# Turning attention's probabilities and all of x with VectorE and DRAM, and making the output projection's second product whole

## The chip, the cores and the metric

The kernel runs on one core of one Trainium2 chip. A core has five engines that run their own instruction queues side by side: TensorE (PE in the profile) multiplies matrices, VectorE (DVE) and ScalarE (ACT) work element by element, GpSimd (POOL) does small work and issues transfers, and SyncE (SP) issues transfers. 16 DMA engines move data between DRAM and the on-chip memory (SBUF). The metric is the device time of one execution in microseconds (us).

## The reference

One layer of a sequence model: 512 tokens of width 2048, all in float32. A norm, a sliding-window attention with a gate, an output projection, a residual, then a second gated branch and a last norm:

```python
hn = rmsnorm(x, norm_g)
q, k, v, gate = split(hn @ w_in)              # 32 heads of 64, 4 key/value heads
scores = q k^T * 64 ** -0.5 + bias            # blocks of 128 queries, 256 keys, window 128
scores = where(mask, scores, min)
m = maximum(scores.max(-1), sink)
e = exp(scores - m)
probs = e / (e.sum(-1) + exp(sink - m))
y = ((probs @ v) * silu(gate)) @ w_out
x = x + y
emb = p @ ple_proj
g = sigmoid(rmsnorm(x, ple_norm) @ ple_gate)
return rmsnorm(x + emb * g, final_g)
```

## The kernel before

**Every large product in three.** A float32 operand is split into a rounded high part (a cast by ScalarE, `fp32r`) and the rest (a subtraction by VectorE). `mm3` (L123 to L128) then issues three matmuls: high by high, high by low, low by high. Weights come in tiles of 128x1024 (512 KB), loaded by SP, split on ScalarE (L109, L765) and VectorE (L110, L766).

**Start (to about 90 us).** x, turned by the host, is scaled and split; the keys, the values and the first two query chunks are projected.

**The attention loop (about 90 to 445 us).** Two things run side by side. `projections` yields one k-step (a `mm3` of 512 columns) at a time for the remaining 14 query and 16 gate chunks, 16 k-steps each. `kinds` holds their order, and `q_at` says where the query chunks stand in it. 464 k-steps fall into the loop. Attention runs in 64 blocks `i`, one per turn of the loop: block `i = 8 d + g` holds four heads (`d`) and 64 queries (`g`). The generator `scores(i)` multiplies queries with keys, adds the bias, takes the maximum, the exponential and the reciprocal, and scales the probabilities into a tile `pr` (L542), queries on partitions. `turn(i)` has TensorE turn them (L551, two transposes of 128x128 a block, one where g is 0, by the identity `ident`), casts the result out of the bank `pt` into `r` (high part on ScalarE, L564; low part on VectorE, L565), and has POOL cut out the keys of the own block (`own`, L575). `weigh(i)` multiplies by the values and adds the result into `U`. In turn `i` of the loop stand the steps of `scores(i)` and `scores(i - 1)`, `turn(i - 2)` and `weigh(i - 3)`; the loop has 67 turns, and the k-steps are shared out over the first 66. The order within a turn is written out by hand for all five engines (`manual_schedule`): after k-steps 0 to 5 stand the weight splits (`W.todo`), the chores (what follows a finished projection) and the next steps of the generators.

**Sums beside the loop.** The output projection and the later `ple_gate` product are computed with seven products of half size in place of eight (numbers 1 to 7), some of which need sums of weight blocks. These sums are made in DRAM during the loop: SP copies a 512 KB block (L723), POOL adds another onto it with an accumulating transfer (L725). `sums_in(i)` shares out these steps.

**The output projection (about 447 to 620 us).** `unit(p, jj, ...)` makes the half `jj` of product `p`: four weight tiles, each 2 k by 2 banks by 3 matmuls. The order is 1, 7, 6, 5, 3, 4 (`ORDER_OUT`). Product 2 is made apart, by the class `Small`, again with seven products of half size, spread over products 3 and 4 (`SMALL["w_out"]`, `small_steps`). `add_y` adds each bank to the resident `x1` (L1120, L1122). The products of the embedding (`EMBED_AT`) stand in between. VectorE and POOL are not ordered by hand in this part; ScalarE is from product 4 on.

**Turning x.** The `ple_gate` product needs the new x with columns on partitions (`hT`). The quarter j of the columns and half th of the tokens goes one of two ways. For j = 0 and 1 with th = 0, `turn(kp, th, tag)` has TensorE transpose 16 pieces of 128x128 (L1054) at the end of product 4. For the others, `turn_blocks` has VectorE transpose blocks of 32x32 (L1073), POOL writes them to DRAM (L1075), `gather_blocks` reads them back in four transfers with the blocks exchanged (L1083), and `scale_turned` scales them on ScalarE (L1092). `turns_at` places these steps.

**The second branch (about 620 to 780 us)** runs the `ple_gate` products in the order 1, 7, 6, 5, 3, 4, its product 2 by `Small`, then the gate and the last norm.

Of the kernel before, what the change touches and what calls it, by code (L numbers as in the profile page):

```python
# [19 lines left out]
S = 512  # L20
P = 128
# [34 lines left out]
def trunk_kernel(ctx: ExitStack, tc: tile.TileContext, a: dict):  # L56
# [75 lines left out]
    ident = const.tile([P, P], F32, name="ident")  # L132
    make_identity(nc, ident)
# [47 lines left out]
    q_at = {int(0.5 + 3.516 * (c // 2)) - 3 + c % 2: c for c in range(2, PAIRS)}  # L181
# [170 lines left out]
    kt = [kvq.tile([P, S], F32, name=f"kt{t}") for t in range(2)]  # L352
# [116 lines left out]
    def scores(i):  # L469
# [64 lines left out]
        T[i] = operands.tile([P, 2, P], F32, tag="pr", name=f"pr{i}", bufs=3)  # L534
        for u in range(2):
            out, src = T[i][:, u], pr[u]
            if g == 0:
                out = T[i][:, 0, u * HB : (u + 1) * HB]
            if late and (g + u) % 2:
                out = out.rearrange("p (h k) -> p h k", h=2)[:, ::-1]  # L540
                src = src.rearrange("p (h k) -> p h k", h=2)
            nc.scalar.mul(out, src, sm[:, 4 + u : 5 + u])  # L542

    def turn(i):


        d, g = divmod(i, UNITS)
        pr = T.pop(i)
        pt = bank(f"pt{i}", "t")[:, :256]
        for u in range(2 if g else 1):  # L550
            nc.tensor.transpose(pt[:, u * P : (u + 1) * P], pr[:, u, :], ident)  # L551

        r = operands.tile([P, 2, 256], F32R, tag="r", name=f"r{i}", bufs=2)
        rh, rl = (r[:, l].rearrange("p (h u q) -> p u h q", h=4, u=2) for l in range(2))
        src = pt.rearrange("p (u h q) -> p u h q", u=2, h=4)
        if g == 0:
            lower, upper = slice(0, HB), slice(HB, P)
            nc.scalar.copy(rh[lower, 0], src[lower, 0])
            nc.scalar.copy(rl[upper, 1], src[upper, 0])
            nc.vector.tensor_sub(rh[upper, 0], src[lower, 0], rh[lower, 0].bitcast(F32))  # L560
            nc.vector.tensor_sub(rh[upper, 1], src[upper, 0], rl[upper, 1].bitcast(F32))
            nc.scalar.copy(rh[lower, 1], rl[upper, 1].bitcast(F32))
        else:
            nc.scalar.copy(rh, src)  # L564
            nc.vector.tensor_sub(rl, src, rh.bitcast(F32))  # L565
# [21 lines left out]
    def weigh(i):  # L587
# [5 lines left out]
        if g == 0:  # L593
            U[d] = apool.tile([P, 2, S], F32, tag="u", name=f"u{d}", bufs=3)
# [14 lines left out]
        if b:  # L609
            dst = U[d][:, :, n * P : (n + 1) * P].rearrange("p u (b q) -> p b u q", b=2)  # L610
            lower, upper = slice(0, 64), slice(64, 128)
            tmp = [apool.tile([P, 2, 2, HB], F32, tag=f"tmp{e}", name=f"tmp{e}_{i}", bufs=1) for e in range(2)]
            for e, (o, x) in enumerate(((lower, upper), (upper, lower))):
                nc.scalar.copy(tmp[e][o], ops[x, :, :, e, :])
            for e, o in enumerate((lower, upper)):
                nc.vector.tensor_add(dst[o], ops[o, :, :, e, :], tmp[e][o])
# [47 lines left out]
    def blk(t):  # L664
# [4 lines left out]
    ORDER_OUT = ORDER_PLE = (1, 7, 6, 5, 3, 4)  # L669

    SMALL = {
        "w_out": {
            (3, 0): {1: [1], 2: [1], 3: [7]}, (3, 1): {0: [7], 1: [6], 2: [6], 3: [2]},
            (4, 0): {0: [2], 1: [5], 2: [5], 3: [4]}, (4, 1): {0: [4, 3], 1: [3]},
        },
# [132 lines left out]
    def add_stage(nm, order):  # L808
        at = {}

        for p in order:
            for jj in range(2):
                at[p, jj] = []
                for m in range(4):
# [3 lines left out]
                    else:  # L818
                        src = block(nm, *{1: (1, 1), 3: (2, 2), 6: (1, 1), 4: (2, 1)}[p], jj, m)
# [8 lines left out]
                    for q in SMALL[nm].get((p, jj), {}).get(m, ()):  # L828
# [21 lines left out]
    class Forms:  # L850
# [6 lines left out]
        def steps(self, p):  # L857

            self.made[p] = []
            for h in range(2):  # L860
# [5 lines left out]
                    5: (a21, (a21, a22)), 3: (a11, (a12, a11)), 4: (a22, None),  # L866
# [52 lines left out]
    def sums_in(i):  # L919
# [6 lines left out]
        n, of = SUM_STEPS - SUMS_EARLY, blocks - 4  # L926
# [9 lines left out]
    for i in range(blocks + 3):  # L936

        before, softmax = softmax, scores(i) if i < blocks else iter(())
        turned = turn(i - 2) if 2 <= i < blocks + 2 else iter(())
        value = weigh(i - 3) if 3 <= i else iter(())  # L940
        next(turned, None)
# [8 lines left out]
        todo = left // (blocks + 2 - i) if i < blocks + 2 else 0  # L950
        left -= todo
        for n in range(max(todo, 6)):
            if n < todo:
                next(proj)
            if n == 0:
                first_chores(i, 1)
                some(W.todo)
                some(chores or idle)
            elif n == 2:
                next(turned, None)  # L960
                next(value, None)
                if len(chores) > 1:
                    some(chores)
            elif n == 3:
                next(softmax, None)
            elif n == 4:
                first_chores(i, 2)
                some(chores or idle)
            elif n == 5:
                next(softmax, None)  # L970
        if i < blocks:
# [19 lines left out]
    def banks(p, jj, nm):  # L991
# [3 lines left out]
        tag = "sp"[jj] if p != 7 else "to"[jj] if nm == "o" else "t"  # L995
# [48 lines left out]
    def turn(kp, th, tag):  # L1044

        g = kp // 2
        if g not in hT:
            hT[g] = swapped[(g + 2) % 4] = quarter(f"hT{g}")
        tp = bank(f"tp{kp}_{th}", tag)
        for n in range(2):  # L1050
            k = 2 * kp + n
            for tb in range(2):
                src = x1[k // 4][:, 2 * th + tb, (k % 4) * P : (k % 4 + 1) * P]
# [784 lines left out]
```

## Time and profile before

| | us |
|---|---|
| median of three runs | 781.91 (781.47 to 781.96) |
| the profiled execution | 781.41 |
| its span, first to last instruction | 779.70 |

Mean granted TensorE clock in that execution: 0.997. The profile is one execution. Each row of its groups of instructions gives the line of the code, the engine, the operation, what it writes and reads with the shapes, how often, the busy time, the mean of one in ns, and the idle time just before. Rows of stretches give start and end, the length, then for each engine the busy time and in brackets the number of instructions (PE, PEld for the loading of the matrix that stands still, DVE, ACT, POOL), the granted clock, the mean busy share of the DMA engines and GB/s. Rows of the chain and of the order in time give start, length, engine, line, operation. Rows of transfers give what is written and read, the issuing queue, the count, the KB of one and the median us from issue to landing. Rows of waits give who waited for whom, the sum, the count and the longest.

### The profile page before, as it was taken

The page shows a single profiled execution, that of the slowest core. Times are in us where ns is not written, and L with a number is a line of the kernel's source. Part 1 is how long each engine was busy: PE and PEld are TensorE (multiplying, and loading weights), DVE is VectorE, ACT ScalarE, POOL GpSimd, SP SyncE. Part 2 cuts the span into 40 slices and gives each one's busy share as a digit, 9 for nine tenths or more (in the row PEclk, how much of TensorE's full clock was granted, in tenths as well). Part 3 has the DMA queues.
Part 4 walks back from the last instruction along what each step waited for, and adds up shares of the span by engine and source line. Part 5 has one row for each costly group of instructions (what it writes and reads, how often), then busy time and mean ns, then how long its engine had stood idle before and what let it go on. Part 6 is the DMA issues. An engine that isn't in the chain of part 4 may idle for free.

```text
span 779.7 us, 11154 instructions
## 1 busy us (share of the span) xinstructions
PE 770.1 (99%) x3652; PEld 644.1 (83%) x3652; DVE 618.9 (79%) x1069; ACT 529.3 (68%) x1121; POOL 169.8 (22%) x307
## 2 busy tenths in 40 slices
PE   9999999999999999999999999999999999999995
PEld 8888888888888888888888888888888888888884
DVE  4546697876978688777877799968799889999995
ACT  6743586766777676766766664577766888867874
POOL 0201523132232313132332200112101122221111
PEclk9999999999999999999999999999999999999998
DMA  9978899999999999999998588999899999999956
GB/s 343 305 207 301 182 260 311 272 312 258 287 247 278 280 241 278 277 279 277 248 288 218 136 298 313 359 290 290 318 389 337 320 284 295 325 264 309 321 132 216
DMA packets 52858, 217.22 MB, mean 279 GB/s; under 512 B 8112, under 2 KB 9136, under 8 KB 46720
## 3 DMA queue, kind: packets, MB, share of 16 engines
q1 hardware_dynamic: 39280, 156.67, 56.5%
q0 software_dynamic: 13520, 59.83, 36.2%
q8 instruction: 29, 0.48, 0.3%
q14 instruction: 29, 0.24, 0.1%
HBM read 199.65 MB, written 82.89 MB: 362 GB/s over the span
## 4 chain that ended last, share of the span: by engine, by line
PE 98%; issue 1%; DVE 0%; POOL 0%; POOLq 0%; DVEq 0%
PE gps L126 7%; PE gps L127 7%; PE gps L128 7%; PE qps L126 7%; PE qps L128 7%; PE qps L127 7%; PE o L126 6%; PE o L127 6%; PE o L128 6%; PE g L127 5%; PE g L128 5%; PE g L126 5%; PE s L485 2%; PE vps L290 2%; PE o L603 2%; PE pt L551 2%
## 5 line engine op out<-in xcount | busy, mean ns | idle before, releaser
L766 DVE TENSOR_TENSOR blo<-braw,bhi 128x1024 fp32r<-128x1024 f32 x100 | 121.5, 1220 | 20.9 <-ACT bhi L765 19.9
L765 ACT CAST bhi<-braw 128x1024 fp32r<-128x1024 f32 x100 | 105.1, 1052 | 47.1 <-PE o L128 15.1
L126 PE MATMUL gps<-xh,whi 128*128 128x512 f32 x256 | 100.0, 390 | 0.0
L127 PE MATMUL gps<-xl,whi 128*128 128x512 f32 x256 | 99.9, 390 | 0.0
L128 PE MATMUL gps<-xh,wlo 128*128 128x512 f32 x256 | 99.8, 390 | 0.0
L126 PE MATMUL qps<-xh,whi 128*128 128x512 f32 x224 | 87.8, 392 | 0.0
L128 PE MATMUL qps<-xh,wlo 128*128 128x512 f32 x224 | 87.5, 390 | 0.0
L127 PE MATMUL qps<-xl,whi 128*128 128x512 f32 x224 | 87.4, 390 | 0.0
L575 POOL TENSOR_SCALAR_AFFINE_SELECT own<-r 64x512 fp32r<-64x512 f32 (+1 forms) x48 | 32.5, 677 | 238.4 <-DVE r L565 234.4
L110 DVE TENSOR_TENSOR wlo<-wraw,whi 128x1024 fp32r<-128x1024 f32 x60 | 73.5, 1227 | 2.8 <-ACT whi L109 2.7
L126 PE MATMUL o<-bhi,fho 128*128 128x512 f32 x192 | 74.8, 390 | 0.0
L127 PE MATMUL o<-blo,fho 128*128 128x512 f32 x192 | 74.7, 389 | 0.0
L128 PE MATMUL o<-bhi,flo 128*128 128x512 f32 x192 | 74.7, 389 | 0.0
L109 ACT CAST whi<-wraw 128x1024 fp32r<-128x1024 f32 x60 | 62.3, 1040 | 4.6 <-issue 4.1
L126 PE MATMUL g<-bhi,fhg 128*128 128x512 f32 x160 | 62.3, 390 | 0.0
L127 PE MATMUL g<-blo,fhg 128*128 128x512 f32 x160 | 62.2, 389 | 0.0
L128 PE MATMUL g<-bhi,flg 128*128 128x512 f32 x160 | 62.2, 389 | 0.0
L128 PEld LDWEIGHTS gps<-xh,wlo 128*128 128x128 f32 x256 | 48.1, 188 | 10.3
L126 PEld LDWEIGHTS gps<-xh,whi 128*128 128x128 f32 x256 | 48.1, 188 | 9.2
L529 ACT ACTIVATE t<-t,sm 128x129 f32<-128x129 f32 (+1 forms) x128 | 49.6, 389 | 8.7 <-DVE sm L525 7.4
L127 PEld LDWEIGHTS gps<-xl,whi 128*128 128x128 f32 x256 | 48.1, 188 | 8.9
L565 DVE TENSOR_TENSOR r<-pt,r 128x256 fp32r<-128x256 f32 x56 | 23.7, 424 | 38.9 <-ACT r L564 38.1
(299 smaller groups left out, 1827.6 us busy)
## 6 DMA issues: line engine op xcount, KB each, us to landing
wraw<-in_w_gate_in SPq DMA_DIRECT2D x32, 512.0 KB, 8.1
w_out<-in_w_out POOLq DMA_DIRECT2D x32, 512.0 KB, 9.1
braw<-w_out SPq DMA_DIRECT2D x32, 512.0 KB, 8.1
wraw<-in_w_q SPq DMA_DIRECT2D x28, 512.0 KB, 6.7
braw<-in_w_out SPq DMA_DIRECT2D x22, 512.0 KB, 5.7
braw<-in_ple_gate SPq DMA_DIRECT2D x22, 512.0 KB, 6.9
ple_gate<-in_ple_gate POOLq DMA_DIRECT2D x20, 512.0 KB, 8.9
xw<-in_first SPq DMA_DIRECT2D x14, 640.5 KB, 6.5
```

The source lines that it names most:

```text
L109: nc.scalar.copy(hi, raw)
L110: nc.vector.tensor_sub(lo, raw, hi.bitcast(F32))
L126: nc.tensor.matmul(ps, sh, mh, start=first, stop=False, skip_group_check=more)
L127: nc.tensor.matmul(ps, sh, ml, start=False, stop=False, skip_group_check=more)
L128: nc.tensor.matmul(ps, sl, mh, start=False, stop=last, skip_group_check=more)
L290: nc.tensor.matmul(v_ps[t], h[:, c], part_of(high_at, 256, 512), start=f, stop=e, skip_group_check=True)
L485: nc.tensor.matmul(s_ps[:, u, : 2 * n], st, of_keys[:, first * 2 * QB : (first * QB + n) * 2], start=True, stop=True)
L529: nc.scalar.activation(su, su, AF.Exp, bias=sm[:, u : u + 1], accum_out=sm[:, 2 + u : 3 + u])
L565: nc.vector.tensor_sub(rl, src, rh.bitcast(F32))
L575: nc.gpsimd.affine_select(out=flat(own), in_=flat(r).bitcast(F32), pattern=[[0, 8], [sign, HB]], compare_op=ALU.is_ge, fill=0.0, base=-HB ...
L765: nc.scalar.copy(hi[:, :n], raw)
L766: nc.vector.tensor_sub(lo[:, :n], raw, hi[:, :n].bitcast(F32))
```

## The change

In attention, `scores` scales the probabilities in place, and a new last step has VectorE transpose them in 32x32 blocks into a tile `turned`, which holds two blocks of attention (a pair `a`). `send(a)` writes it to DRAM from ScalarE's queue (256 KB). `fetch(a)` reads it back on SP's queue in four transfers of 64 KB, in runs of 512 bytes, with the blocks exchanged, into the tile `back`. `turn(i)` casts `r` out of `back` in place of the bank. `weigh` follows seven turns behind `scores` in place of three; the loop has 71 turns, and the k-steps are shared out over 70. `turned` and `back` have two buffers each; to make room `u` has two buffers in place of three (the keys' tile `both_kt` serves as `u` for d = 6) and `tmp` is one tile. `q_at` moves the query chunks earlier. The transposes by `ident`, and `ident` itself, are gone.

In the output projection, product 2 becomes a whole one between products 3 and 4: 8 weight tiles straight from `w_out`. The small products of `w_out`, their sums in DRAM and their forms are gone; the sums that are left are shared out over 64 turns in place of 60. ScalarE is ordered by hand from product 2 on. x is turned for j = 0 and 1, th = 0 too by `turn_blocks`, `gather_blocks` and `scale_turned`; those for j = 2 and 3 move from product 4 to product 2.

```diff
-    q_at = {int(0.5 + 3.516 * (c // 2)) - 3 + c % 2: c for c in range(2, PAIRS)}
+    q_at = {int(0.5 + 3.333 * (c // 2)) - 3 + c % 2: c for c in range(2, PAIRS)}
...
-        T[i] = operands.tile([P, 2, P], F32, tag="pr", name=f"pr{i}", bufs=3)
         for u in range(2):
-            out, src = T[i][:, u], pr[u]
+            nc.scalar.mul(pr[u], pr[u], sm[:, 4 + u : 5 + u])
+        yield
+
+        a, v = divmod(i, 2)
+        if not v:
+            T[a] = operands.tile([P, 512], F32, tag="turned", name=f"turned{a}", bufs=2)
+        to = T[a].rearrange("p (j v u q) -> p v u j q", j=4, v=2, u=2)[:, v]
+        for u in range(2):
+            out, src = to[:, u], pr[u].rearrange("p (j q) -> p j q", q=QB)
...
-            nc.scalar.mul(out, src, sm[:, 4 + u : 5 + u])
+            nc.vector.transpose(out, src)
+
+    apart_of, back = {}, {}
...
+    def send(a):
+
+        apart_of[a] = tc.dram_tile([P, 512], F32, name=f"turned_of{a}")
+        nc.scalar.dma_start(*(within(v.rearrange("p (j x) -> p j x", j=4), a) for v in (apart_of[a], T.pop(a))))
+
+    def fetch(a):
+
+        back[a] = operands.tile([P, 512], F32, tag="back", name=f"back{a}", bufs=2)
+        src = apart_of.pop(a).rearrange("(h k) (j x) -> j k h x", h=4, j=4)
+        for j in range(4):
+            to = back[a][QB * j : QB * j + QB].rearrange("p (h x) -> p h x", h=4)
+            nc.sync.dma_start(within(to, a), within(src[j], a))
 
     def turn(i):
...
-        pr = T.pop(i)
-        pt = bank(f"pt{i}", "t")[:, :256]
-        for u in range(2 if g else 1):
-            nc.tensor.transpose(pt[:, u * P : (u + 1) * P], pr[:, u, :], ident)
-
+        a, v = divmod(i, 2)
+        src = back[a].rearrange("p (h v x) -> p v h x", h=4, v=2)[:, v]
         r = operands.tile([P, 2, 256], F32R, tag="r", name=f"r{i}", bufs=2)
...
-    ORDER_OUT = ORDER_PLE = (1, 7, 6, 5, 3, 4)
+    ORDER_OUT, ORDER_PLE = (1, 7, 6, 5, 3, 2, 4), (1, 7, 6, 5, 3, 4)
...
-        for q in (6, 5) if (nm, p) == ("ple_gate", 5) else (p,):
+        for q in () if nm == "w_out" else (6, 5) if p == 5 else (p,):
             sum_small(nm, q)
...
-        n, of = SUM_STEPS - SUMS_EARLY, blocks - 4
+        n, of = SUM_STEPS - SUMS_EARLY, blocks
...
-    for i in range(blocks + 3):
+    total = left
+    turned = iter(())
+    for i in range(blocks + 7):
 
         before, softmax = softmax, scores(i) if i < blocks else iter(())
-        turned = turn(i - 2) if 2 <= i < blocks + 2 else iter(())
-        value = weigh(i - 3) if 3 <= i else iter(())
-        next(turned, None)
+        value = weigh(i - 7) if 7 <= i else iter(())
...
-        todo = left // (blocks + 2 - i) if i < blocks + 2 else 0
-        left -= todo
-        for n in range(max(todo, 6)):
-            if n < todo:
+        share = total * (i + 1) // (blocks + 6) - total * i // (blocks + 6) if i < blocks + 6 else 0
+        left -= share
+        for n in range(max(share, 6)):
+            if n < share:
                 next(proj)
+            if n == 4 and i % 2 == 0 and 2 <= i <= blocks:
+                send(i // 2 - 1)
+            if n == 2 and i % 2 == 0 and 4 <= i <= blocks + 2:
+                fetch(i // 2 - 2)
+            if n == 2:
+                next(turned, None)
+            if n == 1:
+                next(before, None)
+            if n == 2:
+                next(value, None)
...
+            if n == 2:
+                turned = turn(i - 5) if 5 <= i < blocks + 5 else iter(())
                 next(turned, None)
...
     turns_at = {
...
+        (2, 0, 0): [(turn_blocks, 2, 0)], (2, 0, 1): [(turn_blocks, 3, 0)],
...
+        (4, 0, 0): [(turn_blocks, 0, 0), (scale_turned, 2, 1)], (4, 0, 1): [(scale_turned, 3, 1)],
+        (4, 0, 2): [(gather_blocks, 0, 0), (turn_blocks, 1, 0)], (4, 1, 0): [(gather_blocks, 1, 0)],
+        (1, 0, 0): [(scale_turned, 0, 0), (turn_blocks, 0, 1)],
+        (1, 0, 1): [(gather_blocks, 0, 1), (turn_blocks, 1, 1)],
+        (1, 0, 2): [(gather_blocks, 1, 1), (scale_turned, 1, 0)],
         (1, 1, 2): [(scale_turned, 0, 1)], (7, 0, 1): [(scale_turned, 1, 1)],
     }
```

More of the change, by code (lines that the diff above doesn't have):

```diff
@@ L350, in trunk_kernel @@
         part()
-    kt = [kvq.tile([P, S], F32, name=f"kt{t}") for t in range(2)]
+    both_kt = kvq.tile([P, 2, S], F32, name="kt")
+    kt = [both_kt[:, t] for t in range(2)]
     K = {}
@@ L1042, in trunk_kernel @@
     hT, swapped = {}, {}
[L1044 to L1053, printed above, removed]
-                nc.tensor.transpose(tp[:, (2 * n + tb) * P : (2 * n + tb + 1) * P], src, ident)
-        for n in range(2):
-            k = 2 * kp + n
-            nc.scalar.mul(hT[g][:, k % 4, th * 256 : th * 256 + 256], tp[:, n * 256 : n * 256 + 256], pn[:, k : k + 1])
     SQ = P // 4
@@ L1438, in trunk_kernel @@
         run(nxt)
-        if p == 3:
-            turns = [(kp, 0) for kp in range(4)]
     run(ple_first)
-    assert not turns
     power = const.tile([P, NB], F32, name="power")
```

102 lines of the change are left out of this document (38 added, 64 removed).

## The prediction

> **What bounds the kernel now.** I read the page's totals first, then the chain, then the waits of TensorE.
>
> ```profile
> span 779.7 us, 11154 instructions
> PE 770.1 (99%) x3652; PEld 644.1 (83%) x3652; DVE 618.9 (79%) x1069; ACT 529.3 (68%) x1121; POOL 169.8 (22%) x307
> ...
> PE 98%; issue 1%; DVE 0%; POOL 0%; POOLq 0%; DVEq 0%
> ```
>
> ```profile
> PE warm_ps L141 <- PEq L1828: 0.8, 1, 0.8
> ```
>
> The chain that ended last lies on TensorE for 98% of the span, and the only wait the trace has for TensorE is 0.8 us at the start. A busy PE proves little, since matmuls overlap, so I look at how they follow each other inside one turn of the attention loop (TensorE alone, in order of time):
>
> ```profile
> 248.52 0.39 PE L126 MATMUL gps<-xh,whi 128*128 128x512 f32 x1
> 248.75 0.40 PE L127 MATMUL gps<-xl,whi 128*128 128x512 f32 x1
> ...
> 253.07 0.39 PE L128 MATMUL gps<-xh,wlo 128*128 128x512 f32 x1
> 253.31 0.38 PE L551 MATMUL pt<-ident,pr 128*128 128x128 f32 x2
> 253.44 0.48 PE L603 MATMUL o<-r,V 128*128 128x256 f32 x2
> 253.76 0.28 PE L605 MATMUL o<-own,DV 128*128 128x256 f32 x1
> 253.88 0.46 PE L485 MATMUL s<-k,q 128*128 128x320 f32 x2
> 254.18 0.39 PE L126 MATMUL gps<-xh,whi 128*128 128x512 f32 x1
> ```
>
> From 248.52 to 253.07 lie 20 steps of 0.2275 us: this is the real price of a 512-column matmul (the 0.39 is its overlapped length). From the end of the last one (253.30) to 254.18, 0.88 us go to the two transposes and five attention matmuls. A turn is 254.18 - 248.52 = 5.66 us, with no hole. So the time is the sum of what TensorE issues, as long as everything else keeps up. The next views give what a transpose costs in that sum: the chain between 100 and 440 us by line, the transposes in that stretch, and the chain at the end of the output projection.
>
> ```profile
> by line: PE gps L126 15.3%; PE gps L127 15.2%; PE gps L128 15.1%; PE qps L126 13.4%; PE qps L128 13.4%; PE qps L127 13.4%; PE s L485 4.9%; PE o L603 3.9%; PE pt L551 3.7%; PE o L605 1.6%; PE o L601 0.2%
> ```
>
> ```profile
> 100.00:440.00 340.00, 22.40 (x115) 16.11 (x115) 1.00 0.96 268
> ```
>
> ```profile
> 616.41 0.87 PE tp L1054 x8
> ...
> 620.03 0.87 PE tp L1054 x8
> ```
>
> Attention's transposes: 3.7% of 340 us is 12.6 us over 115, 0.110 us each. The transposes of x: 0.87 / 8 = 0.109 us each.
>
> **The change, part by part.** *Removed from TensorE*: all transposes. Their counts, and those of the output projection, by shape:
>
> ```profile
> L551 PE MATMUL pt<-ident,pr 128*128 128x128 f32 x120 | 23.4, 271 | 0.0
> L1054 PE MATMUL tp<-ident,x1s 128*128 128x128 f32 x16 | 2.1, 272 | 0.0
> L126 PE MATMUL o<-bhi,fho 128*128 128x512 f32 x192 | 74.8, 390 | 0.0
> L126 PE MATMUL smallo<-bhi,small_aho 128*128 128x512 f32 x28 | 10.9, 389 | 0.0
> ```
>
> 120 x 0.110 = 13.2 us and 16 x 0.109 = 1.7 us: -14.9. As upper bound I take the 0.141 us of a transpose's own weight load, in the row below, 136 x 0.141 = 19.2 us; the lower one, that they cost nothing, is rival D.
>
> ```profile
> L551 PEld LDWEIGHTS pt<-ident,pr x120: 138/141/143, 91.4 to 443.9; 128*128 128x128 f32 x120
> ```
>
> The Trainium skill ("VectorE: DVE Perf Modes", Rules for kernel authors) speaks against the change: a 128x128 transpose belongs on TensorE, VectorE turning 32x32 blocks only; its table has 390 ns for one on TensorE alone, by which the sum would be an estimated -50 us. The trace has 271 ns for one and 0.11 us between two, and the trace decides.
>
> *Added to TensorE*: six whole products are 3 x 192 matmuls, so one is 96; the seven small ones it replaces are 3 x 28 = 84. 12 more, 12 x 0.2275 = +2.7 us. The k-steps of the projections stay 464 in the loop, spread over 70 turns instead of 66 (6.63 a turn, not 7.03); `q_at` only reorders them. TensorE's sum is **-14.9 + 2.7 = -12.2 us**.
>
> *VectorE in the loop.* Each block gets two 32x32-block transposes of 128x128. The trace has them only at 128x512:
>
> ```profile
> L1073 DVE STREAM_TRANSPOSE blocks<-x1s 128x512 f32<-128x512 f32 x8 | 5.5, 700 | 0.0
> L1120 DVE TENSOR_TENSOR x1s<-o,x1s 128x512 f32<-128x512 f32 x16 | 10.7, 683 | 0.0
> L516 DVE TENSOR_TENSOR t<-s,t 128x128 f32<-128x128 f32 x8 | 2.2, 281 | 0.0
> L110 DVE TENSOR_TENSOR wlo<-wraw,whi 128x1024 fp32r<-128x1024 f32 x60 | 73.5, 1227 | 2.8 <-ACT whi L109 2.7
> ```
>
> They run like other VectorE work (700 against 683 ns), so I take 0.29 us from the 281 ns row; the bounds are a quarter of 700 (0.18) and 0.70. Two make 0.58 us a turn. The busy time by stretch:
>
> ```profile
> 140.00:380.00 240.00, 240.00 (x1182) 201.64 (x1181) 187.09 (x417) 164.55 (x456) 64.95 (x126) 1.00 0.97 272
> 447.00:620.00 173.00, 173.00 (x771) 143.35 (x770) 150.96 (x183) 114.62 (x164) 24.66 (x39) 1.00 0.95 322
> ```
>
> ```profile
> 460.00:500.00 40.00, 40.00 (x179) 33.10 (x178) 37.51 (x46) 20.36 (x25) 0.00 (x0) 1.00 0.96 345
> ...
> 660.00:700.00 40.00, 40.00 (x178) 33.14 (x177) 38.02 (x46) 30.79 (x45) 9.86 (x13) 1.00 1.01 292
> ```
>
> In the loop VectorE is busy 187.09 / 240 = 78%, 4.41 us of a 5.66 us turn. 0.4 k-steps fewer a turn take off 0.4 x (1.227 / 8 + 3 x 0.69 / 16) = 0.11. With 0.58 that is 4.88 us, in a TensorE turn of 6.63 x 3 x 0.2275 + 0.88 - 0.22 = 5.18 us: 94%. That is tight, but 460 to 500 and 660 to 700 show VectorE at 94 and 95% beside a TensorE without a hole, so the cover can hold and I charge nothing. It also loses a wait: of its 52.9 idle us between 140 and 380, these two stood on the copy out of the transpose's bank, which now reads a tile fetched earlier.
>
> ```profile
> DVE r L565 <- ACT r L564: 26.2, 23, 2.4
> DVE r L560 <- ACT r L559: 9.3, 5, 2.8
> ```
>
> If the cover is gone, each 0.1 us a turn costs 6.4 us over 64 blocks. ScalarE (164.55 / 240 = 69%) has the same copies and scalings, and every second turn issues one `send`: by SP's issues below between 0.33 us (a load) and 0.56 (a quarter of the four bias loads), under 0.3 us a turn, beside TensorE.
>
> *The round trip through DRAM.* `send` waits on ScalarE's queue for the transposes issued three k-steps before; behind it stand the casts of weights and the exponentials. `fetch` waits on SP for the send to land; behind it stand the weight loads and the copies of the sums. The weight loads can bear it: SP already stands 219.8 us on buffers.
>
> ```profile
> SPq L102 <- DVE wlo L110: 219.8, 47, 10.9
> ```
>
> ```profile
> 218.64 0.33 SPq L102 DMA_DIRECT2D wraw<-in_w_gate_in  x1
> 219.02 0.71 SPq L723 DMA_DIRECT2D small_w_out<-small_w_out  x1
> 219.78 2.26 SPq L467 DMA_DIRECT2D bias<-tdram  x4
> ```
>
> A load is issued when the split three tiles back frees its buffer, so it has up to 3 x 8 k-steps x 0.68 = 16 us, and lands in 8.1. What must come in time is the copy `rh`: from `send` (turn 2a+2, fifth k-step) to it (turn 2a+5, third) are 2.7 turns, 2.7 x 5.18 = 14.0 us. The trace shows no such trip; the nearest landings:
>
> ```profile
> wraw<-in_w_gate_in SPq DMA_DIRECT2D x32, 512.0 KB, 8.1
> ...
> out<-x1s SPq DMA_DIRECT2D x14, 256.0 KB, 2.9
> ...
> s<-apart POOLq DMA_DIRECT2D x24, 128.0 KB, 7.1
> ...
> apart<-blocks POOLq DMA_DIRECT2D x4, 512.0 KB, 7.9
> ...
> bias<-tdram SPq DMA_DIRECT2D x32, 20.0 KB, 12.3
> ```
>
> A `send` is 256 KB: between 2.9 (the quiet end of the kernel) and 7.9, I take 5.4. A `fetch` is four gathers of 64 KB in 512 B runs: between 2.9 and 12.3, I take 7.1, the same kind of gather under load. The bias rows are the bad case, issued right behind a load and a copy on one queue; a `fetch` usually has stood waiting for its `send` while these drained. Sum 12.5 us, 1.5 us of slack, and cost nothing.
>
> *Traffic.* Out go eight copies and eight adds of 512 KB (8 MB), in come 32 x 2 x 256 KB (16 MB). From 80 to 447 us about 367 x 0.262 = 96 MB move; 104 MB in 354 us is 294 GB/s, below the 322 that the next stage moves with TensorE full. Nothing charged.
>
> *After the loop.* Whole product 2 splits 8 weight tiles where the small ones took 14: VectorE and ScalarE lose work there. x's first half, j = 0 and 1, takes 4 more transposes of 0.70 us, 2 writes and 8 gathers on POOL, 14% busy there; the gather has six steps of 12 matmuls (16 us) before it is scaled, against 7.1. Nothing charged. Product 4, which now follows product 2, finds its banks freed earlier.
>
> The profiled execution took 781.41 us, 0.5 under the median 781.91. 781.41 - 12.2 = 769.2, by the median **769.7 us**.
>
> **The rivals.** *B, VectorE gives part of it back.* 94% leaves 0.30 us a turn, and ScalarE and VectorE wait for each other several times a turn. For it: about 17 us of its idle time between 140 and 380 (52.9 - 35.5) is not the wait that goes, 0.40 us a turn. If that stays, a turn is 4.88 + 0.40 = 5.28, 0.10 over TensorE's: +6.4, 776.1; double that, about no change. Against it: the 94 and 95% stretches.
>
> *C, the round trip is too long (slower).* Place: the copy `rh` on ScalarE, in the odd turns. It decides from the point where the trip exceeds 14.0 us. ScalarE then stands, VectorE behind it, and both catch up before the next `send` only as fast as VectorE can. Four turns then hold the trip and the 1.3 turns of work from the copy to the next but one `send`: (L + 1.3 x 4.88) / 4. With L = 7.9 + 7.1 = 15.0 a turn is 5.34, +10 us, 780; with L = 5.4 + 12.3 = 17.7 it is 6.0, +53, 823. In between, from L = 15.2, it is slower than before; for the middle, L = 16, 5.59 and +26: 796. Beyond that TensorE runs slower and the queues empty, so it brakes itself. The Trainium skill ("DMA: Bandwidth & Descriptors", Queues, rings and completion order) says that a DMA engine takes the queues in turn packet by packet, which would hold many short runs behind POOL's long accumulates; the bias rows agree, 20 KB in 12.3 us.
>
> *D, it doesn't do what it says.* The 0.88 us is filled by the five other matmuls anyway, so only x's transposes are saved: -1.7 + 2.7, 782.9. Against it: the chain gives the transposes 3.7%.
>
> **How the numbers follow.** Forecast 0.58, its own range 765.5 (0.141 us a transpose) to 773.5. B 0.20, of it 0.04 within 0.2%. C 0.18, of it 0.15 slower, 0.02 the same, 0.01 faster. D 0.04, slower or the same by halves. 0.2% is about what a measurement of this kernel tells from no change. Faster 0.58 + 0.16 + 0.01 = 0.75, same 0.08, slower 0.17. The range must leave out at most 0.2: from 765.5 to 788 it leaves 0.03 below and the worse two thirds of C, 0.12, above.
>
> **What would show it.** Right: no transpose left on TensorE, 224 matmuls on `o` at each of the three lines of `mm3`, a loop turn of about 5.2 us with an unbroken row of 0.2275 us steps, VectorE at 93 to 95% there, STREAM_TRANSPOSE of 128x128 near 0.29 us, send and fetch together under 14 us. B: waits of TensorE on `s` or on a weight split, with VectorE full. C: ScalarE idle before the `rh` copy in `turn`, released by a DMA. Wrong altogether: weight casts that wait for their DMA.

## The result and the profile after

The changed kernel takes **819.44 us** (median of 4 runs, 814.22 to 823.46) against 781.91: ratio 1.048, 95% interval 1.042 to 1.054. It is slower by 37.5 us where the forecast was 12.2 us faster, and outside the forecast's range of 765.5 to 788. The profiled execution took 823.46 us, 4.0 above the median.

From the page: span, busy times, and the chain's shares by engine.

```profile
span 821.7 us, 11390 instructions
...
PE 773.4 (94%) x3528; PEld 640.2 (78%) x3528; DVE 634.0 (77%) x1184; ACT 523.7 (64%) x1112; POOL 161.7 (20%) x307
...
PE 49%; DMA 19%; DVE 13%; ACT 10%; issue 6%; SPq 3%; DVEq 0%; ACTq 0%; POOL 0%; POOLq 0%
```

Before, TensorE held 98% of the chain. Now it holds half, and 19% are transfers. The hole is in the attention loop. The loop as a whole by stretch (start and end, length, busy time of PE, PEld, DVE, ACT and POOL, granted clock, DMA share, GB/s), first before, then after:

```profile
90.00:440.00 350.00, 350.00 (x1721) 294.02 (x1720) 270.90 (x603) 240.40 (x667) 93.73 (x180) 1.00 0.96 268
```

```profile
90.00:440.00 350.00, 318.95 (x1468) 264.25 (x1468) 275.59 (x688) 224.33 (x626) 76.36 (x165) 0.98 0.95 262
```

TensorE lost 31 us of 350. The DMA share did not rise (0.95 against 0.96): SP, which issues the loads, is itself held up, as the next rows show. The last matmul of `o<-own`, which marks the loop's end, starts at 484.2 us; before, it started at 450.2. From there to the end of the span it is 337.5 us (before 329.5).

The planned savings are there: no transpose on TensorE, 224 matmuls on `o` at each line of `mm3`, and VectorE's transpose of 128x128 at 0.288 us (estimated 0.29):

```profile
L126 PE MATMUL o<-blo,fho 128*128 128x512 f32 x224 | 87.5, 391 | 0.5 <-DVE blo L784 0.5
...
L547 DVE STREAM_TRANSPOSE turned<-t 128x128 f32<-128x128 f32 x112 | 28.0, 288 | 0.1
```

What stands instead? From the waits of SP's queue (who, for whom, us in total, times, longest):

```profile
SPq L566 <- DMA turned_of<-turned: 162.2, 24, 13.6
```

This is `fetch` (L566) on SP, waiting for `send` to land. The 219.8 us in which SP stood on weight buffers (`SPq L102 <- DVE wlo L110`, in the prediction) have shrunk to 4.5 us: SP now stands on sends instead, and its loads come late. SP's own order in time shows how, and the chain over the same stretch shows what it costs:

```profile
153.77 0.53 SPq L101 DMA_DIRECT2D wraw<-in_w_q  x1
167.99 1.86 SPq L566 DMA_DIRECT2D back<-turned_of  x4
...
170.52 0.53 SPq L101 DMA_DIRECT2D wraw<-in_w_q  x1
...
171.71 0.53 SPq L101 DMA_DIRECT2D wraw<-in_w_gate_in  x1
```

```profile
154.04 13.87 DMA turned_of<-turned
168.84 0.50 SPq L566
...
170.52 6.47 DMA wraw<-in_w_q
177.07 1.05 ACT whi L108
178.14 1.23 DVE wlo L109
```

From 154 to 168 SP issues nothing. The send takes 13.87 us, then four fetches go, then two weight loads at once, and the cast `whi` starts the moment the first has landed. In the loop (90 to 445 us), the waits that carry this to TensorE:

```profile
DVE wlo L109 <- ACT whi L108: 36.4, 28, 4.1
...
PE o L627 <- ACT own L607: 24.5, 17, 4.5
ACT r L586 <- DMA back<-turned_of: 15.6, 6, 4.2
ACT r L580 <- DMA back<-turned_of: 9.2, 3, 4.1
...
ACT whi L108 <- DMA wraw<-in_w_gate_in: 6.7, 3, 3.5
ACT whi L108 <- DMA wraw<-in_w_q: 6.6, 3, 3.1
```

The largest wait of TensorE is for `own` (24.5 us). In the stretch above it comes from the same late load. The order there, on POOL, ScalarE and TensorE:

```profile
173.86 0.65 POOL L597 TENSOR_SCALAR_AFFINE_SELECT own<-r 64x512 fp32r<-64x512 f32 x1 [9.47 <-DVE r L587]
...
177.07 1.04 ACT L108 CAST whi<-wraw 128x1024 fp32r<-128x1024 f32 x1 [1.88 <-DMA wraw<-in_w_q]
178.13 0.40 ACT L607 CAST own<-own 64x256 fp32r<-64x256 f32 x1
...
178.59 0.58 PE L627 MATMUL o<-own,DV 128*128 128x256 f32 x1 [4.37 <-ACT own L607]
```

POOL has cut out `own` by 174.51. The cast of `own` that ScalarE still has to make stands behind the weight cast `whi` in its hand-written order, and `whi` stands until the load has landed (176.99). TensorE stands 4.37 us for it. So POOL isn't what TensorE waits for here.

Both signs from the prediction's last list are there: C's (the copy in `turn` waits for `back`), and "wrong altogether" (weight casts wait for their DMA). The experiments had to say which matters, and why a send takes 13.87 us.

### The profile page after: what moved, and what is told of

It is laid out like the page before. It is cut to its first block, busy times and chain, and to the rows that moved or that the text cites. A ratio compares the mean times of both kernels' runs of the same rounds, so it can differ in the third digit from the quotient of the medians.

```text
span 821.7 us, 11390 instructions
## 1 busy us (share of the span) xinstructions
PE 773.4 (94%) x3528; PEld 640.2 (78%) x3528; DVE 634.0 (77%) x1184; ACT 523.7 (64%) x1112; POOL 161.7 (20%) x307
## 4 chain that ended last, share of the span: by engine, by line
PE 49%; DMA 19%; DVE 13%; ACT 10%; issue 6%; SPq 3%; DVEq 0%; ACTq 0%; POOL 0%; POOLq 0%
DMA back<-turned_of 7%; PE o L126 6%; PE o L127 6%; PE o L125 6%; DMA turned_of<-turned 5%; ACT whi L108 4%; PE g L126 4%; PE g L127 4%; PE g L125 4%; SPq L566 2%; DVE wlo L109 2%; PE vps L287 2%; DMA wraw<-in_w_q 2%; PE qps L125 2%; PE qps L127 2%
## 5 line engine op out<-in xcount | busy, mean ns | idle before, releaser
L784 DVE TENSOR_TENSOR blo<-braw,bhi 128x1024 fp32r<-128x1024 f32 x94 | 114.7, 1220 | 40.1 <-ACT bhi L783 39.6
L783 ACT CAST bhi<-braw 128x1024 fp32r<-128x1024 f32 x94 | 98.8, 1051 | 66.6 <-PE o L127 27.6
L126 PE MATMUL o<-blo,fho 128*128 128x512 f32 x224 | 87.5, 391 | 0.5 <-DVE blo L784 0.5
L125 PE MATMUL o<-bhi,fho 128*128 128x512 f32 x224 | 87.2, 389 | 0.0
L127 PE MATMUL o<-bhi,flo 128*128 128x512 f32 x224 | 87.2, 389 | 0.0
L533 ACT ACTIVATE t<-t,sm 128x128 f32<-128x128 f32 (+1 forms) x128 | 43.6, 389 | 67.3 <-DVE sm L529 48.5
L127 PEld LDWEIGHTS gps<-xh,wlo 128*128 128x128 f32 x256 | 48.8, 191 | 10.6
```

What stands on the lines that cost most here:

```text
L125: nc.tensor.matmul(ps, sh, mh, start=first, stop=False, skip_group_check=more)
L126: nc.tensor.matmul(ps, sh, ml, start=False, stop=False, skip_group_check=more)
L127: nc.tensor.matmul(ps, sl, mh, start=False, stop=last, skip_group_check=more)
L533: nc.scalar.mul(pr[u], pr[u], sm[:, 4 + u : 5 + u])
L783: nc.scalar.copy(hi[:, :n], raw)
L784: nc.vector.tensor_sub(lo[:, :n], raw, hi[:, :n].bitcast(F32))
```

## The experiments

Five theories. T1: SP stands on the send and the loads behind it are late. T2: the round trip misses the copy `rh` (rival C). T3: VectorE's transposes make the loop late (rival B). T4: the added traffic slows the weight loads. T5: the new output projection loses time. All times below are medians of interleaved runs; the kernel before took 781.75 to 781.94 in each group.

### Without the round trip

`direct`: no `send`, no `fetch`; the casts read `turned` itself (with a third buffer), so the exchange of the blocks is left out.

```diff
-            if n == 4 and i % 2 == 0 and 2 <= i <= blocks:
-                send(i // 2 - 1)
-            if n == 2 and i % 2 == 0 and 4 <= i <= blocks + 2:
-                fetch(i // 2 - 2)
...
-        src = back[a].rearrange("p (h v x) -> p v h x", h=4, v=2)[:, v]
+        src = T[a].rearrange("p (h v x) -> p v h x", h=4, v=2)[:, v]
```

> Attention's send and fetch are left out; the casts read the transposed tile itself, without the exchange of blocks, so the weights on the values are in the wrong places. T1 (the fetch on SP stands waiting for its send, and the weight loads behind it come late) and T2 (the trip itself is longer than its turns, and ScalarE stands before the casts): the loop runs at TensorE's sum, 765 to 775 us. T3 (VectorE at its limit, it and ScalarE wait for each other): still above 800.

Measured 777.26, ratio 0.994 (0.993 to 0.996); the loop ends at 445.2. Of the 49.7 us between the changed kernel and its forecast, 42.2 are gone and 7.6 are left, 2 us more than T1 and T2 allowed. VectorE is at 90% (54.27 of 60 us), where 93 to 95% were forecast:

```profile
200.00:260.00 60.00, 59.22 (x284) 49.86 (x283) 54.27 (x141) 43.72 (x124) 14.45 (x32) 1.00 0.90 254
```

`noturn`: `direct` without VectorE's transposes too; the casts read a constant tile.

```diff
-            nc.vector.transpose(out, src)
...
-        src = T[a].rearrange("p (h v x) -> p v h x", h=4, v=2)[:, v]
+        src = T0.rearrange("p (h v x) -> p v h x", h=4, v=2)[:, v]
```

> As direct, and VectorE's transposes are left out too; the casts read one constant tile, so that attention's output is wrong everywhere. T3 (the 128 transposes on VectorE cost what direct lacked to the sum): 768 to 771. If that loss comes from weight loads that are late at the start of the loop: 775 to 778.

Measured 777.54, 0.994 (0.992 to 0.996): the same. T3 falls as the cause. The transposes aren't quite free, though: between 140 and 380 us TensorE is busy 240.00 us here, and 237.77 in `direct`. Both lose more at the start of the loop (90 to 140 us: 46.17 and 47.42 of 50), which is where this run's second expectation looked for the loss.

### The wait, the deadline and the lag

`fixed`: from the third pair on, `fetch` reads what the second pair has sent (so the wrong probabilities), and needs no newer send. All the traffic stays.

```diff
-        src = apart_of.pop(a).rearrange("(h k) (j x) -> j k h x", h=4, j=4)
+        src = apart_of[min(a, 1)].rearrange("(h k) (j x) -> j k h x", h=4, j=4)
```

> From the third pair on every fetch reads the DRAM tile of pair 1, long landed, so that no fetch waits for a send; all sends and fetches stay, with all their traffic; the probabilities of most pairs are those of another. T1 and T2: 765 to 780. T4 (the traffic of 16 MB delays the weights): above 800. T3: above 800.

794.69, 1.017 (1.014 to 1.020), between its two expectations. 25 us come back, but not the other 17 to `direct`. SP isn't free at the fetch: between 90 and 445 us its stands there add up to 108.5 us (160.6 in the changed kernel), put down to many releasers, 17.8 of them to sends; but none is longer than 6.1 us.

`lagturn1`: casts and weighing one turn later, `fetch` where it was. This gives T2's copy 5 us more.

```diff
-        value = weigh(i - 7) if 7 <= i else iter(())
+        value = weigh(i - 8) if 8 <= i else iter(())
...
-                turned = turn(i - 5) if 5 <= i < blocks + 5 else iter(())
+                turned = turn(i - 6) if 6 <= i < blocks + 6 else iter(())
```

> The casts and the product with the values come one turn later (about 5 us more for the trip), the fetch stays where it was in SP's queue. T2: most of the loss goes, below 795. T1: SP stands as before, the weight loads are as late as before, 810 or more.

822.1, 1.054 (1.049 to 1.058). The casts hardly wait for `back` any more (0.6 us, where it was 24.8), and nothing is gained: the weight casts now do the waiting. T2 falls as the cause.

```profile
ACT whi L108 <- DMA wraw<-in_w_q: 26.7, 12, 4.2
ACT whi L108 <- DMA wraw<-in_w_gate_in: 12.3, 8, 3.9
```

`lag2`: `fetch`, casts and weighing two turns later, so that a send has landed when SP comes to its fetch; the loop gets two turns more.

```diff
-            if n == 2 and i % 2 == 0 and 4 <= i <= blocks + 2:
-                fetch(i // 2 - 2)
+            if n == 2 and i % 2 == 0 and 6 <= i <= blocks + 4:
+                fetch((i - 2) // 2 - 2)
...
+                turned = turn(i - 7) if 7 <= i < blocks + 7 else iter(())
```

> Fetch, casts and the product with the values all come two turns later, so that the send has landed when SP reaches the fetch; nothing else differs. T1 (SP stands for the send before the weight loads): falls to what the run with the fixed source gave, 788 to 800. If the traffic or the short runs of the fetch are the cause of most of the loss (T4): stays above 810.

798.03, 1.020 (1.017 to 1.023); the loop ends at 461.0. SP's wait for sends shrinks from 162.2 us to this:

```profile
SPq L566 <- DMA turned_of<-turned: 19.3, 8, 7.2
```

All its stands at the fetch still add up to 105.4 us (90 to 445), but none is longer than 7.2. So T1 is worth some 21 us here, and again 20.8 us to `direct` are left. The lag has a price of its own, 4.8 us where it is tried without the accumulating transfers (`lag2_noadds` 778.84 and `after_noadds` 774.0, below); with it T1 comes to about the 25 us of `fixed`. Would another queue help? `fetch_act` issues the fetches on ScalarE's queue; `pool_lag2` is `lag2` with POOL issuing them.

```diff
-            nc.sync.dma_start(within(to, a), within(src[j], a))
+            nc.scalar.dma_start(within(to, a), within(src[j], a))
```

> The fetch is issued from ScalarE's queue at the same place, so that ScalarE in place of SP stands for the send. T1: SP's weight loads come in time again, below 795. T2: the trip is as long as it was and ScalarE stands even earlier, 810 or more.

> As the run before it, but the fetch is issued from POOL's queue: SP has its old work alone. T1, with SP's queue of transfers as the whole cause (the fetch in it holds up the weight loads even without a wait): 776 to 786. T4 (the traffic itself): 790 or more.

859.73, 1.100 (1.095 to 1.106), and 812.85, 1.040 (1.036 to 1.044). The first lies in T2's range, but `lagturn1` speaks against T2: with `fetch_act`, ScalarE stands where SP stood, and TensorE waits 42.3 us for its cast of `own` (24.5 in the changed kernel). With `pool_lag2`, SP is free again (90 to 440 us: it stands 220.3 us on weight buffers, as before the change), and the kernel is still 31 us slower than before. So a late place in SP's order isn't all. It isn't a clean test of the traffic either, since POOL, with the fetches, is now busy 108.33 us between 140 and 380 (`lag2` 61.26). The Trainium skill ("DMA: Bandwidth & Descriptors", Issuing engines are not separate DMA queues) says that transfers of any issuer end on the same 16 DMA engines. That other issuers didn't help agrees with it, but doesn't show it.

### The traffic

`direct_traffic`: `direct` with every `send` and `fetch` back, the fetches two turns later and into a tile that nobody reads.

```diff
-        src = back[a].rearrange("p (h v x) -> p v h x", h=4, v=2)[:, v]
+        src = T[a].rearrange("p (h v x) -> p v h x", h=4, v=2)[:, v]
...
-        back[a] = operands.tile([P, 512], F32, tag="back", name=f"back{a}", bufs=2)
+        back[a] = operands.tile([P, 512], F32, tag="back", name=f"back{a}", bufs=1)
```

> The loop of `direct` (the casts read `turned` itself, so nothing waits for the trip), with every `send` and every `fetch` put back, the fetches two turns later and into a tile nobody reads. If the traffic itself costs the 17 us between `fixed` or two turns' lag and `direct` (the DMA queues are full, the weight tiles land late): 792 to 799, weight landings of 8 to 10 us and a DMA share near 1.00. If those 17 us are what is left of waits for the trip: 777 to 780.

794.04, 1.015 (1.010 to 1.019): the 17 us, with no dependence on the trip (its one `back` buffer adds 26.8 us of SP's standing between fetches, so it isn't traffic alone). The weight tiles land in 7.2 and 7.7 us, against 5.4 and 6.7 in `direct`, not quite the 8 to 10 expected. Loop stretch of `direct_traffic`:

```profile
140.00:380.00 240.00, 228.95 (x1060) 190.79 (x1060) 201.18 (x503) 165.25 (x462) 58.17 (x123) 0.98 1.00 282
```

DMA share 1.00, against 0.92 in `direct` (and 1.00 in `fixed` and `lag2`). Now the queues between 140 and 380 us (packets, MB, share of the 16 engines' time), first before, then `lag2`:

```profile
q1 hardware_dynamic: 7967, 42.51, 48.6%
q0 software_dynamic: 3432, 22.47, 48.3%
```

```profile
q1 hardware_dynamic: 20293, 43.79, 52.7%
q0 software_dynamic: 2810, 18.38, 40.3%
```

q0 is POOL's: in the loop these are the accumulating transfers onto the sums of weight blocks. Before the change they already took half of the DMA engines' time for a third of the bytes (22.47 of 65 MB): 5.2 us of all 16 engines per MB, against 2.7 for SP's loads and copies on q1. The two queues left 3% of the time. The forecast had put 16 MB of sends and fetches into that, for 8 MB of sums that go.

`lag2_noadds` and `after_noadds` take the accumulating transfers out of `lag2` and out of the changed kernel; the later products then use the copied blocks without the second summand.

```diff
-        elif i % 2 == 1 and 0 <= i // 2 - 3 < len(adds):
-            nc.gpsimd.dma_start(*adds[i // 2 - 3], accum_op=ALU.add, max_dma_last_dim=8192)
```

> Two turns' lag (798.0), and POOL's accumulating transfers onto the sums of weight blocks are left out in the loop (the later products read the copied blocks alone). These took 40% of the DMA engines' time between 140 and 380 us. If the DMA engines' time is what runs out: the share falls to 0.7 or less, weight landings to 6 us or less, and the time to that of `direct`, 775 to 781. If it is the many short packets of `send` and `fetch` themselves, in whatever room: 790 or more.

> The changed kernel (819.4) with the same accumulating transfers left out. If standing on SP costs by its place in the program whatever the load: about 17 us less, 800 to 804, and SP stands about as long as before. If the sends are only late because the engines are full: SP hardly stands, 777 to 785.

778.84, 0.996 (0.994 to 0.997), and **774.0**, 0.991 (0.989 to 0.994). The changed kernel, with its order untouched, goes from slower by 37 us to faster by 8. Its SP waits and loop stretch:

```profile
SPq L566 <- DMA turned_of<-turned: 164.2, 30, 8.1
```

```profile
140.00:380.00 240.00, 237.69 (x1136) 200.08 (x1135) 213.45 (x539) 174.83 (x491) 31.27 (x93) 1.00 0.69 215
```

SP stands as long as in the changed kernel (164.2 against 162.2 us), but never over 8.1 us at a time, where it was 13.6, and it costs nothing. So standing doesn't cost by its place in the program (that expectation, 800 to 804, fell). The other one, full engines, had the time nearly right, but not that SP would hardly stand. Short packets alone don't explain the loss either: all of them are still there. At the start of the loop, too, TensorE is busy 50.00 of 50 us (90 to 140), where `direct`, without the trip but with the adds, has 47.42. Landings of `after_noadds`, and then of the changed kernel (count, KB of one, median us):

```profile
wraw<-in_w_gate_in SPq DMA_DIRECT2D x32, 512.0 KB, 6.2
...
turned_of<-turned ACTq DMA_DIRECT2D x24, 256.0 KB, 5.4
back<-turned_of SPq DMA_DIRECT2D x96, 64.0 KB, 2.0
```

```profile
wraw<-in_w_gate_in SPq DMA_DIRECT2D x32, 512.0 KB, 9.1
...
turned_of<-turned ACTq DMA_DIRECT2D x24, 256.0 KB, 6.3
back<-turned_of SPq DMA_DIRECT2D x96, 64.0 KB, 5.1
```

Whether it is the engines themselves or the DRAM behind them that is slow can't be told from this: the share counts the time that packets took, whatever held them. No run varies one without the other.

### The output projection

`outonly`: before's loop, with the changed output projection and turning of x. `direct_outb`: the loop of `direct`, with the output projection and turning of x of before.

> The attention loop of before with the output projection, the sums and the turning of x of the changed kernel. By the sum: 12 more matmuls less 16 transposes, +1.0, 783. T5 (the second half of the change stalls by itself; from the end of the loop on the changed kernel was some 8 us longer than before): 786 to 790.

> The loop of `direct` with the output projection, the small products and the turning of x of before. If the changed output projection costs the 4.7 us that `outonly` lost beyond its sum: TensorE's sum rises by 1.7 - 2.7 = -1.0 us and the loss of 4.7 goes, so 777.3 - 4.7 - (-1.0 is already in it) lies between 771 and 774. If that loss came from something that before's loop left behind in `outonly` (its extra small sums are not in it): 776 to 779.

787.53, 1.007 (1.004 to 1.009), where the sum says 781.8 - 1.7 + 2.7 = 782.8; and 775.55, 0.992 (0.990 to 0.993), between its two expectations, 1.7 under `direct`, of which the sum gives 1.0. So T5 is 4.7 us in `outonly` and 0.7 behind the loop of `direct`: small, and not the same behind every loop. In `outonly`, the chain at the end of the output projection shows where, and a wait in 550 to 690 us names it:

```profile
592.30 7.95 DMA s<-apart
600.83 0.34 issue
601.17 0.89 ACT hT L1073 x2
602.07 0.95 ACT bhi L761
```

```profile
ACT hT L1073 <- DMA s<-apart: 4.6, 1, 4.6
```

`scale_turned` stands in ScalarE's hand-written order, waits there for its gather, and the weight cast `bhi` stands behind it.

### Can it be mended?

Three ways with all work done. `sbuf`: one hop in place of two, from `turned` to `back` inside SBUF (12 transfers of 16 KB on SP and 4 on POOL a pair). `sbuf_sp`: all 16 on SP. `sbuf_outb`: `sbuf` with before's output projection.

```diff
-            nc.sync.dma_start(within(to, a), within(src[j], a))
+            for h in range(4):
+                queue = nc.gpsimd if h == j else nc.sync
+                queue.dma_start(
+                    back[a][QB * j : QB * j + QB, P * h + low : P * h + P], src[QB * h : QB * h + QB, P * j + low : P * j + P]
+                )
```

> One hop in place of two: no `send`; the exchange of the blocks goes from `turned` to `back` inside SBUF, 16 transfers of 16 KB a pair (12 on SP, 4 on POOL), casts one turn later. The wait for a landed `send` is gone from SP and a third of the added traffic with it (8 of 24 MB less, counted as written and read once each). If standing on SP and traffic explain the loss: between `direct` (777) and two turns' lag (798), about 788. If the number of issues is what SP cannot bear (12 x 0.47 us in a pair of turns of 10.4 us): loads late again, above 800, with waits of the weight casts on their DMA.

> `sbuf` with before's output projection and turning of x: about 4 to 5 us under `sbuf` if the two parts add, so about 784, and 780 or less if the one hop costs little: the candidate to beat both.

> `sbuf` with all 16 transfers of a pair on SP, none on POOL. If POOL's standing behind the casts was the cause of 1005 us: under 830. If it is the issues themselves (0.65 us each there, 16 x 0.65 = 10.4 us in a pair of turns of 10.4 us): 900 or more, and the weight casts wait for their DMA.

1005.33, 1016.84 and 1066.78 us; before's output projection doesn't help here. POOL's order isn't needed for the loss: without it the kernel is slower still. SP's issues are enough, by its order in time in `sbuf_sp` (of two executions):

```profile
217.49 10.04 SPq L567 DMA_DIRECT2D back<-turned  x16
227.62 0.56 SPq L744 DMA_DIRECT2D w_out<-w_out  x1
228.23 0.58 SPq L101 DMA_DIRECT2D wraw<-in_w_gate_in  x1
```

16 issues take 10.04 us, as long as two turns were meant to take, and the weight load behind them is late (`ACT whi` waited 133 us for the loads between 90 and 445 us). The DMA share there is only 0.58.

`moved`: `lag2`, with the last 32 of 118 steps of the sums (16 of 56 adds; the expectation counted 14) shifted from the loop to products 1, 7, 6 and 5 of the output projection. `moved_nolag`: the same without the lag. `moved48`: `lag2` with 48 steps shifted.

```diff
-        n, of = SUM_STEPS - SUMS_EARLY, blocks
+        n, of = SUM_STEPS - 32 - SUMS_EARLY, blocks
...
+                if p in (1, 7, 6, 5):
+                    for v in more_sums(8 * n + 4 * jj + step):
+                        sum_weights(v)
```

> Two turns' lag, and 32 of the 118 steps of the sums (14 of 56 adds, those needed last) moved out of the loop to products 1, 7, 6 and 5 of the output projection, one step a weight tile; all sums are made. If the DMA engines' time in the loop was what ran out, a quarter of the adds less is 60 us of their time there against some 25 us by which they lacked it: the loop loses most of its 17 us and the time falls to 778 to 785. If the output projection cannot bear the transfers: 790 or more, with TensorE idle between 460 and 570 us.

> The changed kernel without the lag, with the same 32 steps moved. If a late send is only the engines' lack of time, it falls nearly as far as with the lag: 778 to 790. If SP's place in the program costs by itself at this load: near 800.

> Two turns' lag with 48 steps moved (all of the adds for the later product but those of its product 2's first blocks). If the loop still lacked time with 32 moved: some us less than `moved`. If the output projection is then the full one: more than `moved`, with TensorE idle there.

820.02, 1.049 (1.047 to 1.050); 828.01, 1.058 (1.056 to 1.060); 848.39, 1.084 (1.082 to 1.086). The loop does get its time back: it ends at 448.5 with the lag (`lag2` 461.0) and at 462.2 without (changed kernel 484.2). But the output projection pays more than that. `moved`, stretches there:

```profile
490.00:530.00 40.00, 34.88 (x138) 26.73 (x138) 26.88 (x36) 18.23 (x24) 7.22 (x9) 0.96 1.02 332
530.00:570.00 40.00, 31.00 (x114) 23.72 (x115) 20.83 (x24) 21.04 (x32) 9.05 (x13) 0.87 1.03 327
```

```profile
ACT bhi L783 <- DMA braw<-w_out: 36.8, 13, 8.7
```

The engines are as full there, and now its weight tiles are late: between 447 and 620 us `braw<-in_w_out` lands in 9.8 us (5.8 before the change) and `braw<-w_out` in 11.7 (8.1). No kernel that does all the work was faster than the one before.

## Why the prediction was wrong

**TensorE's sum was right to within 5 us.** With the engines relieved (`after_noadds`) the loop ends at 439.6, where 450.2 - 13.2 = 437.0 was forecast, and the whole takes 774.0 against 769.7. What is left lies in the loop (2.6) and behind it: from the loop's end to the span's it is 772.3 - 439.6 = 332.7, where 329.5 - 1.7 + 2.7 = 330.5 was forecast, 2.2 more. So rival D, that attention's transposes cost nothing, falls: without them the loop ends 10.6 us before the old one. Even `direct` (445.2), without any trip, was held up by the adds.

**VectorE was nearly right**: 0.288 us a transpose, 90% busy and not 93 to 95, and `noturn` is no faster than `direct`. Of B some 2 us are left: TensorE's holes between 140 and 380 us are 2.2 us in `direct` and 2.3 in `after_noadds`, and none in `noturn`, each from one execution.

**The step that failed is *Traffic*.** "104 MB in 354 us is 294 GB/s, below the 322 that the next stage moves with TensorE full. Nothing charged." GB/s was the wrong column. The row quoted for VectorE (140 to 380 us, in the prediction) gave the DMA engines' share right beside it: 0.97. An accumulating transfer took more of that time per byte (5.2 us a MB against 2.7), so the stage with many of them was near full at 272 GB/s, and the next one, with few, moves 322. Adding 16 MB for the 8 taken out, in packets two and a half times as many (11418 before, 28685 in `lag2`, 140 to 380 us), went beyond what was there. Counted in engine time the forecast would have seen it. From 80 to 447 us the share is 0.95 of 367 us, 349 us. Eight adds and eight copies less are 4 x 5.2 + 4 x 2.7 = 32 us; 16 MB more, at the 2.8 us a MB of the sends in `lag2` (6.6% of 240 us for 5.56 MB), are 45. That is an estimated 362 us for a loop of 354. Measured: in the loop, 44.6 of the 47.2 us by which it misses its forecast end go when the adds go (484.2, 439.6, 437.0).

**"The weight loads can bear it" failed as a consequence.** SP's 219.8 us on buffers were its lead, and it could be spent as long as no single stand was long. The total says little: between 90 and 445 us SP stands 229 us in the changed kernel, 230 in `lag2` and 224 in `after_noadds`. Of the stands on sends, 164 us in stands of at most 8.1 cost nothing, 162 us in stands of up to 13.6 cost 21 to 25 us (`lag2`, `fixed`). I compared a sum with a sum, where the 16 us that one load has had to be set against one stand plus one landing: 13.6 + 9.1 = 22.7 us here, 8.1 + 6.2 = 14.3 in `after_noadds`.

**The round trip**: send 6.3 and fetch 5.1 us in the median, 11.4 together, within the 12.5 forecast. It is the tail that missed the 14.0 us: the send in the chain above took 13.87 by itself, before its fetch.

**Rival C** had the direction and, by its range (780 to 823), the size; its place was wrong. Stands at the copies in `turn` are 24.8 us in the rows above, and taking them away (`lagturn1`) gained nothing. The bias rows, taken there as a sign of short runs held behind POOL's accumulates, land in 6.1 us in the changed kernel and 6.2 in `direct` (12.3 before), with the accumulates still running; they are no such sign.

**After the loop** nothing was charged; between 2 and 7 us were lost there: 332.7 to 337.5 in `after_noadds` and the changed kernel, against 330.5. Between 550 and 690 us `scale_turned` waits for its gather only 0.8 us in the changed kernel and 2.2 in `after_noadds`, so it isn't most of the 7; the rest wasn't taken apart.

How much is SP's standing and how much late loads can't be split cleanly: the two are one queue, and lag, `fixed` and `direct_traffic` each change both. As far as the runs go, about 25 us go with the waits for sends (`fixed`) and 17 come with the traffic (`direct_traffic`), of the 42.2 between the changed kernel and `direct`.

## What to carry to other kernels

Before a round trip through DRAM is laid beside a stage, read the DMA engines' *share* there and what fills it, not the GB/s: at 0.97, 16 MB more delayed the weights, and the accumulating transfers were the dearest bytes here. A share near 1 doesn't cost by itself: from 660 to 700 us before the change it is 1.01 (in the prediction's rows) with TensorE busy 40.00 of 40 us. Here it left no room for 16 MB more. A transfer that waits for another one on a queue that also prefetches spends the prefetch's lead: compare one stand and one landing, with their worst cases, with the lead of one load. And moving such work to another stage only helps if that stage's engines are not full too.

## Unexpected of the hardware

A late TensorE gets slower. After an idle time of 4.46 us, the matmuls of the changed kernel follow each other in 0.425 us steps ((383.21 - 382.36) / 2) in place of 0.2275, and one lasts 0.63 us in place of 0.39:

```profile
381.44 0.58 PE L627 MATMUL o<-own,DV 128*128 128x256 f32 x1 [4.46 <-ACT own L607]
...
382.36 0.63 PE L125 MATMUL gps<-xh,whi 128*128 128x512 f32 x1
382.78 0.63 PE L126 MATMUL gps<-xl,whi 128*128 128x512 f32 x1
383.21 0.63 PE L127 MATMUL gps<-xh,wlo 128*128 128x512 f32 x1
```

The granted clock is 0.50 between 380 and 386 us and 1.00 again from 392 to 400. Nine matmuls run so, which is about 9 x 0.2 = 1.8 us on top of the hole. So this hole cost more than its length.

The Trainium skill ("TensorE: Matmul & The Clock Gate", HAM oscillation — how this bites in real kernels) has gaps beyond about 3.4 us throttle the clock. The gaps of 4.46 and 4.37 us agree. But between 90 and 500 us of the same execution one of 2.84 us is followed by matmuls of 0.63 us too, and none of 2.36 us or less is; in `lag2` matmuls are slow after gaps of 3.08, 1.93 and 1.30 us and not after 2.77. So by these traces the length of a gap alone doesn't decide it.
